# Placing a projection step between a pair's VectorE products and its ScalarE gelu, and pacing the expert choice by how many rows are left

## The chip, the cores and the metric

The kernel runs on one NeuronCore of one Trainium2 chip. The metric is the device time of one execution in microseconds (us); three executions of the kernel before gave a median of 1524.58 us (1523.93 to 1525.51). All numbers are float32; the projections are computed with operands split into a high and a low part, so that one product becomes three TensorE passes.

## The reference

Two blocks follow each other on 256 tokens of width 1024. The first is a pair of mixers and a mixture of 32 experts, the second is two attentions and a "peer" layer. Only the peer layer is touched here:

```python
q = (xt @ w_q).reshape(t, 8, 2, 128)                 # 8 heads, 2 halves
sc = einsum("thpc,hpnc->thpn", q, sub_keys)          # 128 keys per half
top_s, top_i = top_k(sc, 16)                         # 16 best of each half
cand_s = top_s[:, :, 0, :, None] + top_s[:, :, 1, None, :]
best_s, best_pos = top_k(cand_s.reshape(t, 8, 256), 16)
idx = expert number of best_pos;  gate = softmax(best_s)
act = einsum("cd,ced->ce", x, u[idx])                # 128 experts per token
hid = gelu(act) * gate
out = einsum("ce,ced->cd", hid, v[idx])
```

Each of the 256 tokens reads 128 rows of u and of v, 8 KB together, from tables in HBM. That is 268 MB, half of everything the kernel moves.

## The kernel before, in words

The instruction order on every engine is the order in which the Python code emits instructions; engines run their own queues in order and wait for each other by semaphores. The peer layer starts at about 800 us and has two kinds of work, interleaved by hand.

**Projections.** The 2048 columns of `w_q` come as four loads of 2 MB (`wq0` to `wq3`), issued on SP by `pump` (L331) as soon as an earlier load has been read through (`free`) and a buffer is free. The loop at L1363 does one projection `projT` (L226) per load, i = 0 to 3. A projection has eight steps and a ninth that evacuates it. Each step takes one chunk of 512 columns from `chunk` (L198), which keeps two chunks ahead: it emits ScalarE's copy to the high part `sh` (L164) and the subtraction that gives the low part `sl` (L165; on GpSimd in the first two projections, on VectorE from i = 2 on). Then come the step's twelve matmuls (L234). The ninth step copies the result to `qT` (ScalarE, L125), and `scores` multiplies it with the keys (L1354) and writes `sc` (ScalarE, L1356).

**The choice.** `best` (L1229) and `choose` (L1171) find the experts of four projections' halves: two heads of one tile of 128 tokens, in 14 small steps on VectorE. The last steps are `en` (L1217), the cast to the indices `ei`, and the softmax; the softmax's exponential is on ScalarE (L1207). A finished choice raises `chosen` by 32, that is, by 32 rows. `step` (L1266) emits one step of the first choice on the list `todo`, and then calls `fetch`.

**Rows.** A "row" k (0 to 255) is one of a token tile's 128 expert slots, for all 128 tokens of the tile: an indirect gather of 1 MB, issued on GpSimd (L1263). `fetch` (L1250) issues gathers two at a time (a pair) while the rows are chosen and a buffer is free. There are five buffers of one pair in the ring (and a sixth after the last `w_q` load has been read); a buffer is free for pair p + 5 when `second` of pair p has been emitted, and its gather then waits on the chip for that pair's last matmul.

**What is done with a row.** `first(k)` is VectorE's product of the u half with the tokens, summed along the row (L1294, the tile `jk`, result in `act`). `second(k, 2)` is for a pair: ScalarE's gelu of both sums (L1299), and for each row the gate (L1301) and a diagonal matrix `dg` (L1303); then TensorE adds diagonal times the v half to the four sums `acc` (L1306, eight matmul records a pair).

**The order around the change.** `places` (L1324) emits per pair: the two products, `second`, `fetch`, and yields. `alongside` (L1339) wraps it with one step of the choice before and one after its own yield, so two steps a pair. `drive` (L279) runs a projection and takes one item from `alongside` after each projection step (0.7 items in the second half of i = 1). So with i = 2 and 3 the emitted order is: `sh`, `sl` and matmuls of a projection step; a step of the choice; two products; gelu, diagonals and sums of the same pair; the gather that this pair makes room for; a step of the choice; and so on. 21 of the 128 pairs are emitted beside projections; the rest follow in the loop at L1390 with no projection between them. `final` (L1311) normalises a finished tile of tokens and stores it, after pair 132 and at the end.

Of the kernel before, what the change touches and what calls it, by code (L numbers as in the profile page):

```python
# [59 lines left out]
def body(tc, A, out, dbg=None):  # L60
    with tc.manual_schedule():
        _body(tc, A, out, dbg)


def _body(tc, A, out, dbg):
# [11 lines left out]
    with ExitStack() as ctx:  # L77
# [232 lines left out]
        row_st = {"next": 0, "done": 0}  # L310
# [361 lines left out]
        if True:  # L672
# [70 lines left out]
            with pool("p2b", 2) as q, pool("p2c", 1) as q1:  # L743
# [30 lines left out]
                def places(g):  # L774
                    ahead[g] = Dm = q1.tile([128, 2, 4, 64], F32R, name="Dm")
                    nc.vector.tensor_tensor(Dm, Pp[:, :, 4 * g:4 * g + 4, None].to_broadcast([128, 2, 4, 64]), io64, op=ALU.is_equal)
# [32 lines left out]
                def both(tt, half):  # L809
# [3 lines left out]
                    quarter_sq(yy, ss2, hs, tt, half, "a")  # L813

                places(0)
                weights()
                gather(0)
                pend = None
                pyx = ExitStack()
                for p in range(16):  # L820
# [10 lines left out]
                    if pr == 1 and g < 7:  # L831
                        places(g + 1)
# [415 lines left out]
        chosen = [0]  # L1248
        got = {}
        def fetch():  # L1250

            while row_st["next"] < min(256, chosen[0]):
                k = row_st["next"]

                p = 1 if st["freed"] == len(src) and k % 12 == 10 else 0
                if not space(p):
                    break
                held[p].append(-1 - k // 2)
                w = rg[p].tile([128, 4096], F32, tag="w", name="w")
                for j in range(2):  # L1260
                    tt, s = divmod(k + j, 128)
                    got[k + j] = rw = w[:, j * 2 * D:(j + 1) * 2 * D]
                    nc.gpsimd.indirect_dma_start(rw, None, A["uv"], bass.IndirectOffsetOnAxis(ap=ei[tt][:, s:s + 1], axis=0))  # L1263
                row_st["next"] += 2

        def step():  # L1266
            while todo and next(todo[0], StopIteration) is StopIteration:
                todo.pop(0)
            fetch()

        def filler():
            while True:
                step()
                yield
# [16 lines left out]
        def first(k):  # L1291
            tt, s = divmod(k, 128)
            junk = pj.tile([128, D], F32, name="jk")
            nc.vector.scalar_tensor_tensor(junk, got[k][:, 0:D], 1.0, xr[:, tt], op0=ALU.mult, op1=ALU.mult, accum_out=act[tt][:, s:s + 1])  # L1294

        def second(k, n):
            tt, s = divmod(k, 128)
            v = act[tt][:, s:s + n]
            nc.scalar.activation(v, v, AF.Gelu, scale=r4[:, tt:tt + 1])  # L1299
            for j in range(n):  # L1300
                nc.scalar.activation(v[:, j:j + 1], v[:, j:j + 1], AF.Copy, scale=gf[tt][:, s + j:s + j + 1])  # L1301
                dg = pd.tile([128, 128], F32, name="dg")
                nc.scalar.activation(dg, ident, AF.Copy, scale=v[:, j:j + 1])  # L1303
                rw = got.pop(k + j)
                for hf in range(2):
                    nc.tensor.matmul(acc[tt][hf], dg, rw[:, D + hf * 512:D + (hf + 1) * 512], start=False, stop=(s + j == 127), skip_group_check=True)  # L1306
            row_st["done"] = k + n
# [3 lines left out]
        def final(tt):  # L1311
            scr = pp.tile([128, D], F32, tag=("xh", "res")[tt], name="scr6")
            c = slice(tt, tt + 1)
            for hf in range(2):
                nc.scalar.activation(scr[:, hf * 512:(hf + 1) * 512], acc[tt][hf], AF.Square, accum_out=ss[:, tt, hf:hf + 1])
            nc.vector.tensor_tensor(rfin[:, c], ss[:, tt, 0:1], ss[:, tt, 1:2], op=ALU.add)
            nc.vector.tensor_scalar(rfin[:, c], rfin[:, c], 1.0 / D, EPS, op0=ALU.mult, op1=ALU.add)
            nc.gpsimd.tensor_tensor(rfin[:, c], rfin[:, c], mhalf, op=ALU.pow)
            for hf in range(2):
                v = slice(hf * 512, (hf + 1) * 512)  # L1320
                nc.vector.scalar_tensor_tensor(scr[:, v], acc[tt][hf], rfin[:, c], fg[:, v], op0=ALU.mult, op1=ALU.mult)
                nc.sync.dma_start(out[tt * 128:(tt + 1) * 128, v], scr[:, v])

        def places():  # L1324

            for k in range(0, 256, 2):
                while row_st["next"] <= k + 1:
                    step()
                n = 1 if k == 254 else 2
                for j in range(0, 2, n):  # L1330
                    for i in range(j, j + n):
                        first(k + i)
                    second(k + j, n)
                fetch()
                if k == 132:
                    final(0)
                yield

        def alongside():  # L1339
            for _ in pl:  # L1340
                step()
                yield
                step()


        fill = filler()
        pl = places()
        al = alongside()

        def scores(i, qT, js):  # L1350
            for tt in range(2):
# [201 lines left out]
```

## Time and profile before

| what | before |
|---|---|
| median of the runs | 1524.58 us |
| the profiled execution | 1524.7 us |
| its span, first to last instruction | 1522.9 us |
| TensorE busy, share of the span | 85% |
| VectorE, ScalarE, GpSimd busy | 52%, 33%, 31% |
| mean granted TensorE clock, share of full speed | 0.973 |
| read from HBM over the span | 347 GB/s |
| share of the end chain that is gathers landing | 28% |

The profiled execution is 1.8 us longer than its span. The end chain is the work that ended last, followed back from the last instruction. Where it shows gathers landing, the DMA engines set the time; where it goes from engine to engine, a dependence between them does. The 28% lie almost wholly between 1051 us and 1490 us, where one gather after another is the chain. Before that, from about 850 us to 1051 us, the chain passes between ScalarE, VectorE and TensorE.

### The profile page before, as it was taken

What the parts mean: (1) busy time and instruction counts of PE and PEld (TensorE: products, weight loads), DVE (VectorE), ACT (ScalarE), POOL (GpSimd) and SP (SyncE); (2) the same over time, 40 slices, a digit from 0 to 9 for tenths busy, and PEclk for the clock granted to TensorE, in tenths of its full rate; (3) what the DMA queues carried; (4) which work ended last, traced back from release to release, by engine and by line L of the source; (5) the groups of instructions that cost most, each with busy time, mean ns of one, the idle gap of its engine ahead of it and who ended that gap; (6) DMA issues with size and microseconds to landing.
All of it is one profiled execution on the core that took longest, in us unless ns stands there. A gap on an engine that the chain in (4) does not pass through costs nothing.

```text
span 1522.9 us, 16160 instructions
## 1 busy us (share of the span) xinstructions
PE 1291.2 (85%) x5523; PEld 700.9 (46%) x5523; DVE 791.1 (52%) x1797; ACT 502.3 (33%) x1211; POOL 468.0 (31%) x379
## 2 busy tenths in 40 slices
PE   9899999999899898999996768788777597777776
PEld 7676344434345343988876434433222232222222
DVE  4766123222222223677678465699985454544453
ACT  6645011111111012556653333444433232333322
POOL 1211000000000001243118423345556556665661
PEclk9999999999999999999998989999999999999998
DMA  9517899999999999654115787999999999999995
GB/s 390 221 56 320 348 428 428 426 427 426 428 427 427 428 428 427 247 179 151 77 66 220 292 344 270 357 416 422 420 421 422 421 421 421 421 422 421 422 421 216
DMA packets 57748, 530.22 MB, mean 348 GB/s; under 512 B 6592, under 2 KB 6848, under 8 KB 9408
## 3 DMA queue, kind: packets, MB, share of 16 engines
q0 software_dynamic: 37936, 272.65, 43.7%
q1 hardware_dynamic: 19440, 256.35, 40.4%
q8 instruction: 46, 0.75, 0.2%
q14 instruction: 38, 0.31, 0.1%
q10 hardware_dynamic: 288, 0.16, 0.0%
HBM read 528.08 MB, written 1.05 MB: 347 GB/s over the span
## 4 chain that ended last, share of the span: by engine, by line
DMA 28%; PE 13%; DVE 9%; issue 5%; ACT 3%; POOL 2%; POOLq 0%; DVEq 0%; ACTq 0%; SPq 0%
DMA w<-in_uv_dram,ei 28%; PE b L234 6%; DVE jk L1294 4%; PE acc L1306 3%; PE b L263 1%; PE b L247 1%; POOL w L1263 1%; DVE sl L165 1%; DMA w<-in_w_q_dram 1%; ACT sh L164 1%; DVE en L1217 1%; PE b L1055 1%; DVE oh L1211 1%; ACT dg L1303 0%; PE b L1041 0%
## 5 line engine op out<-in xcount | busy, mean ns | idle before, releaser
L1306 PE MATMUL acc<-w,dg 128*128 128x512 f32 x1024 | 485.1, 620 | 164.4 <-ACT dg L1303 164.0
L1263 POOL DMA_INDIRECT w<-in_uv_dram,ei x256 | 346.6, 1354 | 313.2 <-DMA w<-in_uv_dram,ei 123.8
L1294 DVE SCALAR_TENSOR_TENSOR jk<-w,xr 128x1024 f32<-128x1024 f32 x256 | 315.2, 1231 | 185.9 <-DMA w<-in_uv_dram,ei 184.0
L1306 PEld LDWEIGHTS acc<-w,dg 128*128 128x128 f32 x1024 | 190.6, 195 | 445.3 <-ACT dg L1303 248.5
L842 PE MATMUL b<-w,xg 128*64 128x512 f32 x1024 | 237.8, 605 | 12.1 <-DMA w<-in_w_gate_dram 9.8
L165 DVE TENSOR_TENSOR sl<-w,sh 128x512 fp32r<-128x512 f32 (+1 forms) x185 | 128.9, 703 | 124.2 <-ACT sh L164 123.8
L1299 ACT ACTIVATE act<-act,rr_n 128x2 f32<-128x2 f32 x129 | 38.1, 295 | 391.4 <-DVE jk L1294 391.4
L164 ACT ACTIVATE sh<-w 128x512 fp32r<-128x512 f32 (+1 forms) x208 | 122.3, 603 | 117.5 <-PE b L234 71.8
L842 PEld LDWEIGHTS b<-w,xg 128*64 128x64 f32 x1024 | 82.7, 139 | 155.1 <-issue 132.7
L836 POOL TENSOR_TENSOR Dw<-Dw,Wt 128x256 f32<-128x256 f32 x16 | 9.9, 616 | 391.0 <-DVE Dw L835 391.0
L880 PE MATMUL b<-w,hT 128*64 128x512 f32 x512 | 116.2, 595 | 6.3 <-ACT hT L125 5.5
L234 PE MATMUL b<-nT,sh 128*128 128x256 f32 x576 | 107.9, 288 | 3.3 <-ACT sh L164 1.7
L1303 ACT ACTIVATE dg<-kc,act 128x128 f32<-128x128 f32 x256 | 102.8, 401 | 8.4
L234 PEld LDWEIGHTS b<-nT,sh 128*128 128x128 f32 x576 | 89.8, 192 | 9.4 <-issue 4.7
L804 DVE TENSOR_TENSOR res<-res,b 128x512 f32<-128x512 f32 x64 | 39.9, 683 | 102.1 <-PE b L802 102.1
L234 PE MATMUL b<-nT,sl 128*128 128x256 f32 x288 | 82.3, 286 | 3.1 <-DVE sl L165 2.9
L885 DVE SCALAR_TENSOR_TENSOR eo<-b,gs,eo 128x512 fp32r<-128x512 f32 x32 | 24.0, 751 | 114.3 <-ACT eo L884 111.7
L1301 ACT ACTIVATE act<-act,gt 128x1 f32<-128x1 f32 x256 | 73.4, 287 | 4.2
L880 PEld LDWEIGHTS b<-w,hT 128*64 128x64 f32 x512 | 41.3, 137 | 68.7 <-issue 58.7
L849 DVE TENSOR_TENSOR hs<-hs,b 128x512 f32<-128x512 f32 x16 | 11.0, 688 | 105.2 <-PE b L842 105.2
L884 ACT ACTIVATE eo<-b,gs 128x512 fp32r<-128x512 f32 x32 | 22.0, 686 | 114.6 <-PE b L880 88.0
L247 PE MATMUL b<-sh,nT 128*128 128x512 f32 (+1 forms) x192 | 58.2, 379 | 0.5 <-ACT sh L164 0.5
(373 smaller groups left out, 1410.9 us busy)
## 6 DMA issues: line engine op xcount, KB each, us to landing
w<-in_w_gate_dram SPq DMA_DIRECT2D x32, 2048.0 KB, 20.2
w<-in_w_up_dram SPq DMA_DIRECT2D x32, 2048.0 KB, 21.1
w<-in_w_down_dram SPq DMA_DIRECT2D x32, 2048.0 KB, 19.1
w<-in_w_in_dram SPq DMA_DIRECT2D x13, 2048.0 KB, 16.3
w<-in_w_out_dram SPq DMA_DIRECT2D x4, 2048.0 KB, 13.1
w<-in_w_q_dram SPq DMA_DIRECT2D x4, 2048.0 KB, 9.8
w<-in_uv_dram,ei POOLq DMA_INDIRECT x256, 19.1
w<-in_w_in_dram SPq DMA_DIRECT2D x4, 512.0 KB, 7.2
```

What stands on the lines that cost most here:

```text
L164: nc.scalar.activation(hi, src, AF.Copy)
L165: (eng or nc.vector).tensor_tensor(lo, src, hi.bitcast(F32), op=ALU.subtract)
L234: nc.tensor.matmul(dst, l[:, c * 128:(c + 1) * 128], x[:, r, k, :], start=(k == 0 and c % 2 == 0 and i == 0), stop=(k == nk - 1 and i == 2 ...
L247: nc.tensor.matmul(bs[tt][:, :n], x[:, l, k, tt * 128:(tt + 1) * 128], r[:, :n], start=(k == 0 and i == 0), stop=(k == 7 and i == 2))
L804: nc.vector.tensor_tensor(rs, rs, b, op=ALU.add)
L842: nc.tensor.matmul(dst[64 * j:64 * j + 64, :], xg[:, k, 2 * pr + j, :], w[j][:, k * 512:(k + 1) * 512], start=(k == 0), stop=(k == 7))
L880: nc.tensor.matmul(bh[half][64 * j:64 * j + 64, :], hT[:, f, 64 * j:64 * j + 64], w[j][:, f * 1024 + half * 512:f * 1024 + half * 512 + 51 ...
L1263: nc.gpsimd.indirect_dma_start(rw, None, A["uv"], bass.IndirectOffsetOnAxis(ap=ei[tt][:, s:s + 1], axis=0))
L1294: nc.vector.scalar_tensor_tensor(junk, got[k][:, 0:D], 1.0, xr[:, tt], op0=ALU.mult, op1=ALU.mult, accum_out=act[tt][:, s:s + 1])
L1301: nc.scalar.activation(v[:, j:j + 1], v[:, j:j + 1], AF.Copy, scale=gf[tt][:, s + j:s + j + 1])
L1303: nc.scalar.activation(dg, ident, AF.Copy, scale=v[:, j:j + 1])
L1306: nc.tensor.matmul(acc[tt][hf], dg, rw[:, D + hf * 512:D + (hf + 1) * 512], start=False, stop=(s + j == 127), skip_group_check=True)
```

## The change

`places` now yields after a pair's two products and before its `second`, so that whatever the caller emits next (a projection step) stands between them in the queues. `alongside` is gone; `places` itself emits the steps of the choice, after `second` and `fetch`: three where fewer than 16 chosen rows are left that have not been fetched, otherwise one. The last pair is emitted row by row as before.

```diff
@@ places
             for k in range(0, 256, 2):
                 while row_st["next"] <= k + 1:
                     step()
-                n = 1 if k == 254 else 2
-                for j in range(0, 2, n):
-                    for i in range(j, j + n):
-                        first(k + i)
-                    second(k + j, n)
+                if k == 254:
+                    for j in range(2):
+                        first(k + j)
+                        second(k + j, 1)
+                    return
+                first(k)
+                first(k + 1)
+                yield
+                second(k, 2)
                 fetch()
                 if k == 132:
                     final(0)
-                yield
-
-        def alongside():
-            for _ in pl:
-                step()
-                yield
-                step()
+                for _ in range(3 if chosen[0] - row_st["next"] < 16 else 1):
+                    step()
 
 
         fill = filler()
-        pl = places()
-        al = alongside()
+        al = places()
```

## Rows read from the trace of the kernel before

**Rows 1.** Stretches: us, busy us (x instructions) by engine, PEclk, DMA share, GB/s

```profile
842.00:986.00 144.00, 111.63 (x417) 64.73 (x415) 82.55 (x240) 51.16 (x128) 47.62 (x46) 0.91 0.81 317
985.00:1490.00 505.00, 379.06 (x816) 148.84 (x816) 322.41 (x768) 176.27 (x531) 290.36 (x204) 0.98 1.01 421
```

**Rows 2.** Shorter stretches of the same view, inside the first

```profile
862.00:866.00 4.00, 4.00 (x5) 1.70 (x6) 3.53 (x15) 0.92 (x2) 0.00 (x0) 0.50 0.00 0
910.00:914.00 4.00, 4.00 (x6) 1.42 (x6) 3.90 (x7) 1.58 (x5) 0.00 (x0) 0.50 0.01 2
934.00:938.00 4.00, 4.00 (x6) 1.55 (x5) 3.90 (x17) 0.64 (x3) 0.00 (x0) 0.51 0.00 0
...
958.00:974.00 16.00, 14.82 (x49) 8.17 (x49) 14.33 (x24) 6.57 (x21) 6.29 (x6) 0.89 0.81 296
```

**Rows 3.** Chain that ended last, 869 to 901 us: start, length, what

```profile
869.12 0.64 ACT sh L164
...
870.79 1.16 DVE jk L1294 x2
871.96 1.25 DVE jk L1294 x2
...
874.51 0.40 ACT dg L1303
874.91 0.53 ACT sh L164
...
889.97 10.91 DMA w<-in_w_q_dram
```

**Rows 4.** ScalarE's timeline: start, length, instruction, idle before and its releaser

```profile
855.14 0.62 ACT L164 ACTIVATE sh<-w 128x512 fp32r<-128x512 f32 x1
...
888.57 0.61 ACT L164 ACTIVATE sh<-w 128x512 fp32r<-128x512 f32 x1
...
900.96 0.63 ACT L164 ACTIVATE sh<-w 128x512 fp32r<-128x512 f32 x1 [6.03 <-DMA w<-in_w_q_dram]
906.70 0.29 ACT L1299 ACTIVATE act<-act,rr_n 128x2 f32<-128x2 f32 x1 [5.11 <-DVE jk L1294]
...
925.28 0.62 ACT L164 ACTIVATE sh<-w 128x512 fp32r<-128x512 f32 x1
...
959.41 0.61 ACT L164 ACTIVATE sh<-w 128x512 fp32r<-128x512 f32 x1
```

**Rows 5.** TensorE's timeline: sums of single pairs, and a projection's scores

```profile
837.41 3.70 PE L1306 MATMUL acc<-w,dg 128*128 128x512 f32 x8 [1.28 <-ACT dg L1303]
...
842.38 3.60 PE L1306 MATMUL acc<-w,dg 128*128 128x512 f32 x8
...
907.81 6.77 PE L1306 MATMUL acc<-w,dg 128*128 128x512 f32 x8 [8.31 <-ACT dg L1303]
...
922.71 1.95 PE L1354 MATMUL b<-ky,qT 128*128 128x128 f32 x16
```

**Rows 6.** GpSimd's timeline: gathers that were issued late

```profile
867.99 0.94 POOL L1263 DMA_INDIRECT w<-in_uv_dram,ei  x1 [12.79 <-DVE cand L1183]
...
914.85 0.94 POOL L1263 DMA_INDIRECT w<-in_uv_dram,ei  x1 [14.33 <-PE acc L1306]
...
938.90 0.94 POOL L1263 DMA_INDIRECT w<-in_uv_dram,ei  x1 [13.57 <-PE acc L1306]
```

**Rows 7.** VectorE's groups from 850 to 985 us: busy us, mean ns, idle before

```profile
L1294 DVE SCALAR_TENSOR_TENSOR jk<-w,xr 128x1024 f32<-128x1024 f32 x36 | 43.9, 1220 | 0.7
L165 DVE TENSOR_TENSOR sl<-w,sh 128x512 fp32r<-128x512 f32 x14 | 9.7, 692 | 52.4 <-ACT sh L164 52.4
...
L1217 DVE TENSOR_REDUCE en<-oh 128x32 f32<-128x1600 f32 x2 | 3.6, 1816 | 0.0
L1294 DVE DVE_READ_ACCUMULATOR jk<-w,xr 128x1 f32 x36 | 3.0, 83 | 0.0
```

**Rows 8.** DMA issues by line: KB each, median us to landing

```profile
w<-in_w_gate_dram SPq DMA_DIRECT2D x32, 2048.0 KB, 20.2
...
w<-in_w_q_dram SPq DMA_DIRECT2D x4, 2048.0 KB, 9.8
```

**Rows 9.** VectorE's timeline: a product while GpSimd does L165

```profile
831.16 2.30 DVE L1294 SCALAR_TENSOR_TENSOR jk<-w,xr 128x1024 f32<-128x1024 f32 x1
```

## The prediction

> **What bounds the kernel now.** I read first the stretches of the span. From 985 us to the last gather the DMA engines are busy throughout and move 421 GB/s [rows 1]; nothing emitted in another order makes that part shorter, since the bytes stay the same. A pair of rows is 2 × 128 × 8 KB = 2.10 MB, so at that rate it takes 4.98 us. The 144 us before it, where pairs run beside the projections, reach only 317 GB/s [rows 1]. Against 421 GB/s this loses 144 × (1 − 317/421) = 35.6 us. That is all this change can win, and only through gathers that start earlier. The shorter stretches show where it goes: three times the engines stand at 0.00 or 0.01 of their time, and from 958 to 974 us they reach 296 GB/s [rows 2].
>
> Next the GpSimd timeline, which issues the gathers: each hole follows a gather that came 12.8 to 14.3 us late, two of them put down to the sums of the pair whose buffer was needed [rows 6]. (The first is put down to a VectorE instruction, but its gather needs a pair's sums in the same way.) So the ring is full and the DMA waits for pairs to be consumed.
>
> Then the chain, to see what paces consumption. From one copy `sh` to the next it goes ScalarE, VectorE, ScalarE: copy at 869.12, products from 870.79 to 873.2, last diagonal at 874.51, next copy at 874.91, 5.79 us [rows 3]. It closes because VectorE's products stand behind the `sl` that needs the copy, and ScalarE's next copy stands behind the gelu that needs the products. Neither engine is full: VectorE idled 52.4 us for `sh` in 135 us [rows 7].
>
> **The part that breaks the loop.** After the change ScalarE has the copy of the next chunk ahead of a pair's gelu, and VectorE has the pair's products ahead of that chunk's `sl`. While VectorE multiplies pair p, ScalarE can do the diagonals of pair p − 1 and the next copy. The added wait, the gelu behind a copy, has the pair's diagonals and sums queued behind it, and the gather of pair p + 5 waits for those. No instruction or DMA is added or removed. What follows is worked out with three cycle times. TensorE: sums of two pairs with a projection step between them started 4.97 us apart [rows 5]. The DMA: 4.98 us. VectorE: two products 2.41 us [rows 3], `sl` 0.69 us, and choice steps. In the 144 us VectorE was busy 82.55 us [rows 1]; less products, accumulator reads and `sl` [rows 7] 25.9 us is left for some 28 choice steps, 0.9 us each. That gives 4.0 us with one step and 5.8 us with three.
>
> Term 1, the first boundary (second projection to third, 837 to 855 us). One pair's sums, 3.70 us [rows 5], no longer stand ahead of the scores on TensorE, so the third projection starts that much earlier, less a share that ScalarE's other order takes: 1 to 3.7 us, taken 3.
>
> Term 2, third projection up to its last copy of `wq2`. Five cycles now take 888.57 − 855.14 = 33.4 us [rows 4]. Counting `chosen` and fetched rows by the loops, the first of these pairs has 16 rows left (one step) and the next four 14 down to 8 (three steps): 4.97 + 4 × 5.8 = 28.2 us. The heavy steps fall in them (`en` alone 1.82 us [rows 7]), which I bound with 30.5 us. Gain 3 to 5 us, taken 4.
>
> Term 3, the last weight load. It starts when `wq2` has been read through, and takes 10.91 us [rows 3]; ScalarE stands still for it, for 6.03 us beyond its other work [rows 4]. The order keeps one cycle between the last copy of `wq2` and the first of `wq3`, so the load is exposed as before. Its length among denser gathers isn't shown. The bounds are 9.8 us (median of these loads) and 20.2 us (median of an expert's load of the same size [rows 8]); I take 10.91, nearest in place, and price the other end as a rival. What changes is what comes after: now `sl`, a choice step and two products follow the copy, and the gelu comes at 906.70, 5.74 us behind the copy's start at 900.96 [rows 4]. Afterwards the products are already there, and the gelu is 0.6 us behind. From this copy to the first of the fourth projection it is 24.3 us now [rows 4]. In its place stand 0.6 us for the copy, 1.1 us from the gelu to the first sum (906.70 to 907.81 [rows 4, 5]), three pairs of sums, a projection step (4.97 − 3.6, about 1.4 us), 1.95 us of scores and 0.6 us from their end to the copy (925.28 − 924.66). The sums take 3 × 3.7 us, or 6.77 + 2 × 3.7 where the first runs at the half clock that they show now after an idle TensorE [rows 2, 5]. That is 16.8 to 19.8 us. Gain 4.5 to 7.5 us, taken 5.5.
>
> Term 4, fourth projection. Five cycles take 959.41 − 925.28 = 34.1 us [rows 4]. By then 20 to 30 chosen rows are left, so one step a pair: VectorE's 4.0 us lies beside TensorE's 4.97, 24.9 us for five. With 5.3 us a cycle for imperfect meshing it is 26.5. Gain 7.6 to 9.3 us, taken 8.5.
>
> Term 5, the projection's end. After 974 us the DMA is nearly full already, so here only the hole of 958 to 974 us can be won: 16 × (1 − 296/421) = 4.75 us [rows 2]. Between 0 and that; taken 4.5, as the end comes some 20 us sooner.
>
> Term 6, against the change. When the projections end, one pair fewer has been released than now, because `second` comes one projection step later: −4.98 us.
>
> The sum is 3 + 4 + 5.5 + 8.5 + 4.5 − 5 = 20.5 us. The lower ends give 1 + 3 + 4.5 + 7.6 + 0 − 5 = 11.1 us, the upper ones 3.7 + 5 + 7.5 + 9.3 + 4.75 − 5 = 25.3 us. It is made against the profiled execution's 1524.7 us, which is 0.1 us from the median.
>
> **What I cost at nothing.** In the tail, without projections, the queues differ from now only by one or three choice steps in place of two a pair. VectorE is busy 322 of 505 us there and the DMA is full [rows 1], which hides it. The cover is gone if the choice runs late: counting by the loops, fewer than 10 unfetched rows (25 us of gathers) remain only among the first eight pairs, where three steps a pair catch up, and at the end, when all are chosen. The way from the last landing to the end is unchanged.
>
> **The rivals.** First, *consumption stays the bound*. For it: a third of the pairs beside projections get three steps, VectorE then needs 5.8 us or more, and TensorE drops to half clock after each hole [rows 2]. Then term 2 is 0, term 3 its lower end, term 4 with 5.7 us a cycle 5.6, term 5 3: 3 + 0 + 4.5 + 5.6 + 3 − 5 = 11.1 us, 1513.6 us. Against it: VectorE's idle time for `sh` [rows 7] shows room.
>
> Second, *the last load lands late*, because the gathers beside it are denser. At 20.2 us [rows 8] the stall is 9.3 us longer and the gain 11.2 us: 1513.5 us. Against it: a full ring can't hold more than five pairs, now as then.
>
> Third, *nearly all is recovered*: consumption runs ahead, only the load's stall remains, 35.6 − 7.5 = 28 us, 1496.5 us.
>
> Fourth, *nothing changes*: the gathers would be bound by the DMA anyway, 1524.5 us. The stretches with a share of 0.00 [rows 2] speak against it.
>
> Fifth, the *slower* side: VectorE's products take 2.30 us in place of 1.22, as one did while GpSimd worked on L165 [rows 9]. Then a pair needs 2.1 us more of VectorE. Five cycles of the third projection get 10.5 us longer; eight of the fourth need 4.6 + 0.7 + 0.9 = 6.2 us in place of 4.97, 9.8 us; three pairs between, 3.6 us. That is 24 us, 3.5 us more than the gain: 1528 us. It decides where a product's mean passes about 2.1 us. Against it: GpSimd has no L165 left in that stretch, and 36 products beside gathers took 1220 ns [rows 7]. The Trainium skill (SBUF — State Buffer, Who interferes with whom) states that a VectorE instruction with two SBUF inputs contends with a GpSimd instruction that reads SBUF, and not with one that only writes it; by that rule products slow down beside L165 and not beside the gathers' descriptors, and the trace agrees at 2.30 and 1.22 us.
>
> **How the numbers follow.** Chances: the forecast 0.57, consumption-bound 0.2, late load 0.08, nearly all 0.07, nothing 0.04, slower 0.04. The predicted time is 1524.7 − 20.5 = 1504.2 us. The forecast's own ends are 1499.4 and 1513.6 us. The range goes past them on the slow side to take in the first two rivals, and on the fast side to within 0.5 us of the third: 1497 to 1515 us. About 0.2% (3 us) is what a measurement of this kernel tells from no change: faster 0.92, same 0.04, slower 0.04.
>
> **What would show it.** Right: from 842 to about 960 us a rate near 380 GB/s and no 4 us without DMA save around the last load; ScalarE's gelu waiting for products almost nowhere in that stretch; copies of the fourth projection about 5 us apart; the last scores near 955 us, 27 us earlier than now; a tail of 421 GB/s that is shifted whole. Wrong: copies still 6 us or more apart, VectorE idle less but TensorE at half clock, a load of 15 us or more, or holes in the tail's DMA share.

## The result and the profile after

The changed kernel takes 1506.47 us (median of four executions, 1505.81 to 1509.5) against 1524.49 us: a ratio of 0.9885, 95% interval 0.9868 to 0.9902, 18 us less. The forecast was 1504.2 us, in a range of 1497 to 1515.

Its profiled execution took 1509.5 us, the longest of the four, with a span of 1507.6 us. It came to its first gather at 819.54 us, the profiled one of before at 816.62 us, although nothing differs up to there. So I compare times counted from the first gather: from it to the end of the span it is 1522.9 − 816.62 = 706.3 us before and 1507.6 − 819.54 = 688.1 us after, 18.2 us less. The two ways of counting agree.

The stretches of the changed kernel, with the columns of [rows 1]:

```profile
842.00:846.00 4.00, 2.98 (x7) 1.44 (x8) 1.17 (x2) 2.01 (x6) 3.55 (x4) 1.00 0.03 8
900.00:904.00 4.00, 3.88 (x5) 1.81 (x6) 3.97 (x7) 2.75 (x9) 0.00 (x0) 0.50 0.87 350
904.00:908.00 4.00, 4.00 (x17) 2.37 (x17) 3.76 (x7) 0.80 (x2) 1.10 (x2) 0.85 0.01 2
...
842.00:960.00 118.00, 103.26 (x397) 60.50 (x398) 81.34 (x230) 50.86 (x131) 51.73 (x45) 0.96 0.91 354
842.00:986.00 144.00, 125.82 (x460) 71.05 (x460) 103.41 (x315) 62.13 (x165) 66.06 (x57) 0.96 0.93 366
...
985.00:1475.00 490.00, 364.07 (x780) 142.73 (x778) 302.69 (x694) 168.58 (x506) 304.23 (x196) 0.98 1.01 421
1209.54:1219.54 10.00, 10.00 (x24) 4.37 (x23) 9.89 (x16) 5.93 (x20) 6.37 (x6) 1.00 0.95 381
```

The tail is what it was, 421 GB/s, but for one dip: from 1209.54 to 1219.54 us it moves 381 GB/s, which loses 0.9 us; around the same rows the kernel before has no 10 us under 418 GB/s. The 144 us before it now move 366 GB/s where they moved 317 [rows 1]; what is lost against 421 GB/s fell from 35.6 us to 144 × (1 − 366/421) = 18.8 us, and the difference of 16.8 us is nearly the whole gain. Two of the three holes of [rows 2] are gone, the one behind the last load is still as empty (0.01 of the time from 904 to 908 us), and one is new (842 to 846 us).

The chain in the third projection no longer alternates between ScalarE and VectorE as in [rows 3]. Here are its subtractions, products and the heavy choice step, and the load that follows:

```profile
878.75 0.08 DVE jk L1294
878.83 0.60 DVE sl L165
879.43 0.91 DVE oh L1211
...
881.40 1.83 DVE en L1217
...
883.35 1.24 DVE jk L1294 x2
...
885.84 0.61 DVE sl L165
...
886.51 11.90 DMA w<-in_w_q_dram
```

From one `sl` to the next it is VectorE alone, 7.0 us in this heaviest cycle: VectorE paces. In the fourth projection the chain is TensorE alone:

```profile
918.65 3.70 PE acc L1306 x8
922.35 1.43 PE b L234 x12
923.78 3.67 PE acc L1306 x8
927.45 1.44 PE b L234 x12
928.88 3.44 PE acc L1306 x8
...
943.49 3.44 PE acc L1306 x8
```

Five cycles take 943.49 − 918.65 = 24.8 us, TensorE's own work and nothing else.

On ScalarE the gelu now follows the awaited copy at once, where it came 5.74 us after it in [rows 4]:

```profile
885.88 0.29 ACT L1299 ACTIVATE act<-act,rr_n 128x2 f32<-128x2 f32 x1 [4.82 <-DVE jk L1294]
...
898.49 0.63 ACT L164 ACTIVATE sh<-w 128x512 fp32r<-128x512 f32 x1 [10.93 <-DMA w<-in_w_q_dram]
899.02 0.28 ACT L1299 ACTIVATE act<-act,rr_n 128x2 f32<-128x2 f32 x1
...
917.03 0.62 ACT L164 ACTIVATE sh<-w 128x512 fp32r<-128x512 f32 x1
```

TensorE's first sums behind that stall, after 6.32 us without work, still run at the lower clock (granted 0.50 from 900 to 904 us, that is, 1.2 of 2.4 GHz), and the later ones at the full one (1.00 from 906 to 910 us), as in [rows 5]:

```profile
900.12 6.21 PE L1306 MATMUL acc<-w,dg 128*128 128x512 f32 x8 [6.32 <-ACT dg L1303]
...
918.65 3.70 PE L1306 MATMUL acc<-w,dg 128*128 128x512 f32 x8 [0.81 <-ACT dg L1303]
```

Of the gathers on GpSimd, only one pair is still more than 10 us late (three in [rows 6]); the first row below is the new hole, where four gathers stand behind three subtractions of the projection:

```profile
837.79 6.51 POOL L165 TENSOR_TENSOR sl<-w,sh 128x512 fp32r<-128x512 f32 x3 [0.24 <-ACT sh L164]
844.44 0.95 POOL L1263 DMA_INDIRECT w<-in_uv_dram,ei  x1
...
906.60 0.94 POOL L1263 DMA_INDIRECT w<-in_uv_dram,ei  x1 [11.76 <-DVE jk L1294]
...
927.72 1.13 POOL L1263 DMA_INDIRECT w<-in_uv_dram,ei  x1 [2.46 <-PE acc L1306]
```

The last of these is row 34. It comes 108.2 us after the first gather; before it was 122.3 (938.90 [rows 6] − 816.62). VectorE's idle time for `sh`, in the shorter stretch from 850 to 960 us, columns as in [rows 7]:

```profile
L1294 DVE SCALAR_TENSOR_TENSOR jk<-w,xr 128x1024 f32<-128x1024 f32 x36 | 44.0, 1223 | 0.7
L165 DVE TENSOR_TENSOR sl<-w,sh 128x512 fp32r<-128x512 f32 x14 | 9.6, 688 | 33.6 <-ACT sh L164 33.6
```

The same 36 products and 14 subtractions, as fast as before, with 33.6 us of waiting in place of 52.4.

### The profile page after: what moved, and what is told of

The parts are those of the page before. It is cut to its first block, busy times and chain, and to the rows that moved or that the text cites. A ratio compares the mean times of both kernels' runs of the same rounds, so it can differ in the third digit from the quotient of the medians.

```text
span 1507.6 us, 16162 instructions
## 1 busy us (share of the span) xinstructions
PE 1288.7 (85%) x5523; PEld 697.2 (46%) x5523; DVE 792.0 (53%) x1797; ACT 502.0 (33%) x1211; POOL 496.2 (33%) x379
## 4 chain that ended last, share of the span: by engine, by line
DMA 36%; PE 24%; DVE 6%; issue 5%; POOL 2%; ACT 2%; POOLq 0%; DVEq 0%; ACTq 0%; SPq 0%
DMA w<-in_uv_dram,ei 30%; PE b L234 6%; PE b L842 6%; DMA w<-in_w_gate_dram 6%; PE acc L1306 4%; PE b L880 2%; POOL w L1263 2%; DVE jk L1294 1%; PE b L263 1%; PE b L247 1%; PE b L802 1%; DVE sl L165 1%; DMA w<-in_w_q_dram 1%; PE b L788 1%; PE b L1055 1%
## 5 line engine op out<-in xcount | busy, mean ns | idle before, releaser
L1263 POOL DMA_INDIRECT w<-in_uv_dram,ei x256 | 374.6, 1463 | 266.0 <-DMA w<-in_uv_dram,ei 134.6
L165 DVE TENSOR_TENSOR sl<-w,sh 128x512 fp32r<-128x512 f32 (+1 forms) x185 | 128.7, 702 | 107.3 <-ACT sh L164 106.8
L842 PEld LDWEIGHTS b<-w,xg 128*64 128x64 f32 x1024 | 78.9, 139 | 158.9 <-issue 138.7
```

Source lines behind the costliest of these rows:

```text
L165: (eng or nc.vector).tensor_tensor(lo, src, hi.bitcast(F32), op=ALU.subtract)
L842: nc.tensor.matmul(dst[64 * j:64 * j + 64, :], xg[:, k, 2 * pr + j, :], w[j][:, k * 512:(k + 1) * 512], start=(k == 0), stop=(k == 7))
```

## The experiments

Every run is compared with the kernel before in the same session. Because the time up to the first gather wanders by some us from one execution to the next, each also has the time from the first gather to the end in its profiled execution ("the peer layer": 706.3 us before, 688.1 us with the change); that is the sharper number of the two for small differences. Two things in it are not the edits' doing. Row 14 comes 40.4 us after the first gather in some profiled executions and 41.9 in others that don't differ up to there. And the kernel's last sums run at two speeds; here they are first in the order alone, then in the kernel with the half clock taken out (both below):

```profile
1487.59 8.83 PE L1306 MATMUL acc<-w,dg 128*128 128x512 f32 x16 [2.22 <-ACT dg L1303]
...
1486.53 7.13 PE L1306 MATMUL acc<-w,dg 128*128 128x512 f32 x16 [2.24 <-ACT dg L1303]
```

The granted clock in the 4 us from 18 us after the last gather is 0.57 in the first and 1.00 in the second; what decides it no run here shows. The way from the last gather to the end takes 34.0 to 34.2 us in eight of the profiled executions, those of before and after among them, and 32.4 to 32.5 us in five. Those five are marked below and compared by the time from the first gather to the last: 672.2 us before, 653.9 us with the change, 649.3 us with the order alone.

### Which half of the change does it

The order alone, with two steps a pair as before the change:

```diff
-                for _ in range(3 if chosen[0] - row_st["next"] < 16 else 1):
+                for _ in range(2):
                     step()
```

> The new order alone: the yield stands between the products and the gelu, but every pair emits two steps of the choice, as before the change. My theory (pairs are consumed at the pace of the busiest engine; three steps make that VectorE in the third projection, order does the rest): VectorE needs 2.41 + 0.69 + 1.8 = 4.9 us a pair, so five cycles of the third projection take about 25 us in place of the 29.2 us of the changed kernel, all later gathers come about 4 us sooner: about 1502.5 us. Rival (pacing by need carries half of the gain): about 1515 us.

Measured 1502.22 us, ratio 0.9845 (0.9828 to 0.9861), peer layer 683.4 us. The pacing alone:

```diff
                 first(k + 1)
-                yield
                 second(k, 2)
...
                     step()
+                yield
```

> The pacing alone: gelu, diagonals and sums right behind the products as before, then three steps or one, then the yield. My theory (the loop from ScalarE's copy over VectorE's products back to ScalarE stays closed, but no step stands between the subtraction and the products any more): a cycle is 0.69 + 2.41 + 1.6 + 0.6, about 5.4 us in the fourth projection and 5.8 in the third where there are three steps, against 6.8 and 6.7 us before; with 1.8 us behind the last load that is 11 to 13 us: about 1512.5 us. Rival (only the order breaks the loop, pacing is worth nothing): 1522 us or more.

Measured 1515.66 us, ratio 0.9932 (0.9915 to 0.9949), peer layer 696.6 us. So in the peer layer the order alone brings 706.3 − 683.4 = 22.9 us, the pacing alone 9.7 us, and both together only 18.2 us: on top of the order, the pacing by three or one costs 4.7 us. The reason stands in VectorE's timeline. These are the subtractions of the third projection in the run with the order alone:

```profile
857.11 0.69 DVE L165 TENSOR_TENSOR sl<-w,sh 128x512 fp32r<-128x512 f32 x1 [13.41 <-ACT sh L164]
863.75 0.69 DVE L165 TENSOR_TENSOR sl<-w,sh 128x512 fp32r<-128x512 f32 x1
868.58 0.69 DVE L165 TENSOR_TENSOR sl<-w,sh 128x512 fp32r<-128x512 f32 x1
...
882.26 0.69 DVE L165 TENSOR_TENSOR sl<-w,sh 128x512 fp32r<-128x512 f32 x1
```

Five cycles take 25.2 us, as expected. In the changed kernel the first and last of them start at 856.54 and 885.76, 29.2 us. From the second pair on, though, it is TensorE and no longer VectorE that has no gap there: its sums start 4.86 to 4.96 us apart. The chosen rows wouldn't have run out without the hurry: with two steps a pair the gathers are as regular.

Why pacing alone helps the old order at all is seen in its chain in the fourth projection:

```profile
934.64 0.64 ACT sh L164
...
935.34 0.57 issue
935.91 1.24 DVE jk L1294 x2
937.17 1.25 DVE jk L1294 x2
938.44 0.30 ACT act L1299
```

No choice step stands any more between the subtraction and the products. In this projection it was 1.58 to 3.09 us from the copy to the products in the kernel before, 2.19 on average, the longest from the copy at 925.28 [rows 4] to this product:

```profile
928.37 1.21 DVE L1294 SCALAR_TENSOR_TENSOR jk<-w,xr 128x1024 f32<-128x1024 f32 x1
```

Now it is 1.25 to 1.27 us. That is 0.9 of the 1.3 us by which a cycle gets shorter there (6.83 to 5.55 us from copy to copy). The steps have moved behind the products, beside ScalarE's work. The loop itself stays closed: copy, subtraction, products, gelu.

### Is time lost where the DMA engines stand still, or where pairs are consumed late?

The new hole at 842 us can be made smaller without touching consumption:

```diff
                 first(k + 1)
+                fetch()
                 yield
```

> The changed kernel with one more call of fetch between the products and the yield, so that the gathers of rows 8 and 9 stand ahead of a GpSimd subtraction that now delays them by about 3 us (the DMA engines stand still from 842 to 846 us in the changed kernel's profile). My theory (gathers are released by consumed pairs; a gather that comes sooner early on only waits longer in its buffer): no change, 1506.5 us within 1 us. Rival (every us in which the DMA engines stand still is lost): about 3 us less, 1503.5 us.

Measured 1506.59 us, ratio 0.9873 (0.9857 to 0.989), peer layer 688.0 us. Rows 8 and 9 came 2.1 us sooner (22.8 us after the first gather in place of 24.9) and the DMA share of that stretch rose from 0.03 to 0.37, but row 14 moved by 0.3 us, row 34 and the end not at all. The filled hole comes back as a lower rate behind it. These are the first and second 40 us from the first gather, in the changed kernel and then in this one:

```profile
819.54:859.54 40.00, 29.70 (x153) 22.37 (x152) 23.23 (x71) 14.62 (x32) 29.28 (x22) 0.91 0.86 339
859.54:899.54 40.00, 30.11 (x116) 17.51 (x114) 29.67 (x89) 13.79 (x35) 14.08 (x12) 0.94 0.95 369
...
820.25:860.25 40.00, 29.36 (x153) 21.98 (x152) 23.54 (x71) 14.10 (x31) 29.31 (x22) 0.91 0.89 352
860.25:900.25 40.00, 29.83 (x116) 17.44 (x114) 28.98 (x88) 13.11 (x33) 14.05 (x12) 0.93 0.93 357
```

Together they move as much (339 + 369 and 352 + 357 GB/s). So lost DMA time isn't free: in the first 200 us from the first gather the rate is 335 GB/s before, 376 with the change, 383 with the order alone and 358 with the pacing alone, which against 421 GB/s loses 40.9, 21.4, 18.1 and 29.9 us, and these differ as the peer layers do, to within 1.5 us. But a hole that is filled without pairs being consumed sooner only moves.

### The stall for the last weight load

Without the load (the fourth projection uses the third's weights; `again` is a new argument that keeps the tile):

```diff
-        src += [A["w_out2"][i] for i in range(2)] + [A["w_q"][i] for i in range(4)]
+        src += [A["w_out2"][i] for i in range(2)] + [A["w_q"][i] for i in range(3)]
...
-        for i in range(3):
-            plan(list(granule()))
+        plan(list(granule()))
+        plan(list(granule(last=False)))
+        plan(list(granule(again=True)))
```

> The changed kernel without the last 2 MB load of the query weights: the fourth projection reads the third's weights again, so its heads' choice is another one. My theory (the stall of ScalarE and VectorE for that load delays all later pairs one for one): the first copy of the fourth weights comes about 9.6 us sooner and the sums after it run at full clock, 2.5 us more; 12 us in all: about 1494.5 us. Rival (the stall hides behind gathers under way, only the load's own 2.1 MB at 421 GB/s count): 5 us, 1501.5 us.

Measured 1496.86 us, ratio 0.9808 (0.9791 to 0.9825), peer layer 678.3 us, 9.8 us less than the changed kernel: below the 12 expected, and twice the 5 us of its bytes. Row 26 comes 77.8 us after the first gather in place of 87.1.

Next, the half clock behind the stall, with the order and two steps:

```diff
-                drive(projT(8, n4, keep(qT, 0)), al, 1)
+                main = projT(8, n4, keep(qT, 0))
+                drive(itertools.islice(main, 6), al, 1)
+                if i == 2:
+                    warm(28)
+                drive(main, al, 1)
```

> The order with two steps a pair (1502.2 us), and 28 matmuls of zeros on TensorE ahead of the projection step that waits for the last weight load, so that TensorE isn't idle in that stall. My theory: the first sums behind the stall then run at full clock, 3.7 us in place of 6.2, and every later pair comes 2.5 us sooner: about 1499.7 us. Rival (the half clock there is absorbed by pairs that wait for data): 1502.2 us.

The kernel before took 1524 to 1530 us beside this run, and by the times nothing can be told: 1502.72 us, ratio 0.9846 (0.9811 to 0.988). The peer layer took 681.0 us, 2.4 less than with the order alone, but this is one of the five: its last gather came only 0.8 us sooner (648.5 us after the first). The timeline of TensorE:

```profile
887.74 6.21 PE L111 MATMUL b<-zero 128*128 128x512 f16 x28
896.99 3.70 PE L1306 MATMUL acc<-w,dg 128*128 128x512 f32 x8 [1.61 <-ACT dg L1303]
```

With the order alone it was:

```profile
896.99 5.53 PE L1306 MATMUL acc<-w,dg 128*128 128x512 f32 x8 [7.42 <-ACT dg L1303]
```

The first sums take 3.70 us at a granted clock of 1.00 (896 to 901 us), in place of 5.53 at 0.50 (896 to 900 us); the 6.21 us of my expectation were the changed kernel's. From the awaited copy (895.36 us in both) to the first copy of the fourth projection it is 16.91 us in place of 17.87. So the trace shows 1 us gained, less than half of what I expected, and the timed runs show nothing.

The load can also be moved rather than removed:

```diff
-        for i in range(3):
-            plan(list(granule()))
+        for i in range(2):
+            plan(list(granule()))
+        plan(list(last_granule()))
...
+                wx[0] = pp.tile([128, 2048], F32, tag="res", name="wx")
+                nc.sync.dma_start(wx[0], A["w_q"][3][:, 0:2048])
                 continue
```

(`last_granule` reads chunks 0 to 3 from `wx`, and 4 to 7 from the usual buffer, for which the list of loads has the second half only.)

> The order with two steps a pair, and the last weight load split: its first half goes at 820 us into the 1 MB of the residual, which is no longer read then; its second half goes where the whole went. Nothing is left out. My theory (the stall delays all later pairs one for one, its bytes cost nothing while the DMA engines have holes): as without the load, some 10 us less, about 1492.5 us. Rival (the bytes and their place in the queues count): 1499 us or more.

Measured 1494.89 us, ratio 0.9792 (0.9759 to 0.9825), peer layer 675.2 us, 8.2 us less than with the order alone. The bytes are all there, and no copy waits for that load any more, so the stall was the price, with the half clock behind it. With this, the 144 us stretch is nearly full:

```profile
842.00:986.00 144.00, 128.15 (x474) 71.34 (x473) 122.36 (x376) 67.18 (x175) 70.55 (x59) 1.00 0.99 404
```

### Which engine paces which projection

Five products are done twice, in one kernel in the third projection and in another in the fourth (`24 <= k <= 32`):

```diff
                 first(k + 1)
+                if 6 <= k <= 14:
+                    first(k + 1)
                 yield
```

> The changed kernel with one product done twice in each of five pairs of the third projection (rows 6 to 15; the result is the same). My theory (with three steps VectorE paces that projection): 5 x 1.3 us = 6.5 us more from the first gather to the end, about 694.5 us in place of 688.1, and as much in the time. Rival (ScalarE or TensorE paces it): under 2 us more.

> The changed kernel with one product done twice in each of five pairs of the fourth projection (rows 24 to 33). My theory (TensorE paces it at 4.97 us a pair, and VectorE with one step has 4.0 us of work): 5 x (5.3 - 4.97) = about 1.7 us more, 689.8 us from the first gather to the end in place of 688.1. Rival (VectorE paces it too): 6.5 us more, 694.5 us.

The first took 1510.47 us, ratio 0.9904 (0.9882 to 0.9927), peer layer 691.9 us; the second 1506.28 us, 0.9869 (0.9843 to 0.9894), 687.9 us. In both profiled executions row 14, ahead of the edit, came 1.5 us sooner after the first gather than in the changed kernel's (40.4 and 41.9 us), and both are among the five. From row 14 to the last gather they are 7.1 and 3.1 us longer; the times alone tell neither from the noise. Here are the subtractions of the third projection in the first kernel:

```profile
851.85 0.69 DVE L165 TENSOR_TENSOR sl<-w,sh 128x512 fp32r<-128x512 f32 x1 [10.69 <-ACT sh L164]
...
887.30 0.69 DVE L165 TENSOR_TENSOR sl<-w,sh 128x512 fp32r<-128x512 f32 x1
```

Five cycles take 35.5 us in place of 29.2: the five products cost their full length, 6.2 us. And the sums of the fourth projection in the second kernel's chain:

```profile
913.63 3.70 PE acc L1306 x8
...
941.64 3.44 PE acc L1306 x8
```

Five cycles take 28.0 us in place of 24.8: the same amount of VectorE work costs 3.2 us there, half of its length, between the two expectations. The first two cycles are the long ones, 6.38 and 6.10 us. So VectorE paces the third projection, and TensorE the fourth, where VectorE has some 0.6 us a pair to spare, half of a product.

With that, two steps where rows are short and one elsewhere should be the better pacing:

```diff
-                for _ in range(3 if chosen[0] - row_st["next"] < 16 else 1):
+                for _ in range(2 if chosen[0] - row_st["next"] < 16 else 1):
```

> The changed kernel with two steps in place of three where fewer than 16 rows are left, otherwise one. My theory (VectorE paces where it has more than 2.4 + 0.7 + 1.8 us a pair, TensorE's 4.97 us otherwise): the third projection as with two steps, the fourth as in the changed kernel: 1 to 2 us less than with two steps throughout, about 1501 us. Rival (only the count in the third projection matters): 1502.2 us.

Measured 1500.59 us, ratio 0.9826 (0.98 to 0.9851). The time looks as I expected, but the peer layer took 683.4 us, exactly as with two steps throughout; this profiled execution had its first gather 4.6 us sooner. So the rival is right here, at the end. On the way rows 36 to 60 came 2 to 6 us sooner, but some 1 us of it was left from row 92 on and nothing in the last 70 rows; from 380 to 400 us after the first gather, the place of the dip in the changed kernel's tail, this kernel moves 405 GB/s and the order alone 422. Together with the half load sent early I expected the two pacings to be equal again:

> The half load sent early, with two steps where fewer than 16 rows are left and otherwise one. My theory: as the half load with two steps throughout, 675 us from the first gather to the end within 1 us, since the two pacings were equal there, and some 1494 us. Rival (without the stall the pacing counts again, as the fourth projection is reached sooner): 2 us or more less, 673 us.

Measured 1494.75 us, ratio 0.9794 (0.9772 to 0.9815), peer layer 673.6 us. That is 1.6 us less than with two steps throughout, but this is one of the five: the last gather comes 641.2 us after the first in place of 641.1. So the two pacings are equal here too, as my theory said.

### The first boundary

The old order for the first three pairs:

```diff
                 first(k)
                 first(k + 1)
-                yield
+                if k >= 6:
+                    yield
                 second(k, 2)
...
-                for _ in range(2):
-                    step()
+                step()
+                if k < 6:
+                    yield
+                step()
```

> The order with two steps a pair, but the first three pairs (second projection) keep the old order, so that their gathers aren't held back by a projection step. My theory (term 1: what counts at the first boundary is that the scores stand ahead of one pair's sums): the third projection starts about 2 us later again and the time is about 1504.5 us. Rival (the pair that is released later, and the hole of the DMA engines from 842 us on, cost more than the earlier scores bring): 3 us less, 1499 us.

Measured 1505.03 us, ratio 0.9861 (0.9835 to 0.9887), peer layer 684.8 us, 1.4 us more than with the order alone. Row 14 comes 4.0 us sooner (37.9 in place of 41.9), rows 16 and 24 4.5 us later, and the last gather 3.0 us later (652.3 in place of 649.3; this is the last of the five). The sign is the theory's, its size a little above the 2 us expected; the timed difference is within the noise.

## Why the prediction was right, point by point

**What bounds the kernel.** Right. The tail stayed at 421 GB/s but for its dip, and the gain lies in the stage beside the projections, by gathers that are released sooner. The lost DMA time that the prediction counted is the right sum. That it can only be won by releasing gathers sooner was argued in the prediction; the added `fetch`, whose hole only moved, and the load that was moved with all its bytes show it.

**Term 1**, 3 us expected (1 to 3.7). From the first gather to the first copy of the third projection it was 855.14 − 816.62 = 38.5 us and is 855.88 − 819.54 = 36.3: 2.2 us. The prediction had no place for the GpSimd queue here, where the gathers of rows 8 to 11 now stand behind one more subtraction; row 8 comes 3.2 us later than before. The added `fetch` takes back 2.1 us of that and gains nothing at the end.

**Term 2**, 4 us expected (3 to 5): 33.4 − 29.2 = 4.2 us. Right, with its reason: VectorE paces with three steps. What I didn't draw from it is that the three steps themselves are the cost; at two steps the same cycles take 25.2 us.

**Term 3**, 5.5 us expected, load unchanged. The load took 11.90 us in place of 10.91, 1 us against it, and from the awaited copy to the first of the fourth projection it was 18.5 us in place of 24.3, a gain of 5.8. Net 4.8.

**Term 4**, 8.5 us expected: 34.1 − 24.8 = 9.3 us, from copies before to sums after. The upper end; TensorE has no gaps between its pairs. From sums to sums it was 965.32 − 931.99 = 33.3 us before, so 8.5 us.

**Terms 5 and 6**, together −0.5 us expected. This is the mis-sized part. The first four terms come to 20.5 us as measured, and I had 21. But the whole is 18.2, so −2.3 us are left. Of these, some 0.8 us lie in the tail, which I had costed at nothing: the changed kernel's rows are 18.7 to 19.5 us ahead from row 92 to row 144 and 18.2 to 18.3 over the last 70, with the dip to 381 GB/s in between; what opens it was not tested. The rest arises before row 92. Row 44 comes 20.1 us sooner (152.6 to 132.5 us after the first gather), rows 54 to 70 even 24 to 26 us. But from 980 us on the DMA engines of the kernel before move 420 GB/s or more almost throughout, so an issue that comes sooner than it did there is no DMA time won. How the rest divides between terms 5 and 6 no run here shows.

**The signs to look for.** Copies of the fourth projection 5 us apart, and a tail that is shifted whole but for those 0.8 us: seen. The others were wrong. From 842 to 960 us I expected a rate near 380 GB/s, and it is 354. The last scores start at 959.92 us in place of 982.42, 22.5 us earlier (25.4 counted from the first gather) and not 27. I expected the gelu to wait for products almost nowhere; it waits up to 4.82 us in the third projection and up to 2.90 in the fourth, harmlessly, since VectorE and TensorE set the pace there and ScalarE is early. And I expected no hole but the one around the load; there is the one at 842 us.

**The rivals.** *Consumption stays the bound* was half right: it does, VectorE in the third projection and TensorE in the fourth, but with shorter cycles. *The load lands late*: by 1 us, not 9. *Nearly all is recovered*: 18.8 us are still lost, a good part of them to the load's stall. The *slower* side needed products of over 2.1 us; they took 1223 ns on average.

## What to carry to other kernels

Where two engines hand work to each other in turns and both take their queues in order, look in the chain for a loop between them; emitting the next item's first half ahead of this item's second half opens it, and then the busiest engine paces. After that count the small work per item on that engine: what was harmless filler in the loop is on the path once the loop is open, so keep it below the pace of the next busiest engine (here two steps a pair, not three). And in a ring of buffers price what a delay does to the release of the buffers: a DMA hole that is filled without releasing them sooner comes back later. The remaining stall, 8.2 us with the bytes kept, was worth more than the pacing. For differences of 1 or 2 us compare the traces between the same two points, and look at what lies outside them.

## What was not expected of the hardware

The same instructions up to the first gather took from 814.5 to 820.3 us in the profiled executions of the changed kernel and its eleven variants, and 816.6 us in the one of before. No run here was made to find out why; it stays open, and it is as large as some of the effects above.

A gather's instruction on GpSimd takes 0.94 us by itself and up to 1.9 us beside VectorE's products, here in the tail of the changed kernel, two gathers behind each other:

```profile
1406.90 1.35 POOL L1263 DMA_INDIRECT w<-in_uv_dram,ei  x1 [1.14 <-DMA w<-in_uv_dram,ei]
1408.85 1.88 POOL L1263 DMA_INDIRECT w<-in_uv_dram,ei  x1 [0.60 <-DMA w<-in_uv_dram,ei]
```

The products next to them keep their 1.22 us. Here the one that waits is the gather, while beside GpSimd's subtractions it is the product (2.30 us [rows 9]). The Trainium skill (SBUF — State Buffer, Who interferes with whom) names a shared pair of ports between the two engines and says that a product with two SBUF inputs contends with GpSimd's reads; the longer gathers fit if issuing one includes such reads, which no run here separates.
